# A gate projection in seven half-size products, its left operands made by quarters of x, in a hybrid decoder block on Trainium2

## The chip, the cores and the metric

The kernel runs on one core of one Trainium2 chip. The metric is the device time of one execution in microseconds. TensorE (PE in the profile; PEld is its weight load) multiplies, VectorE is DVE, ScalarE is ACT, GpSimd is POOL, SyncE is SP. Each engine works through its own queue in order. SP, ACT and POOL also issue DMA transfers.

## The reference

One decoder block over 512 positions of width 1024, in float32: a normalised input goes through one large projection, a short gated convolution and an mLSTM, whose outputs are merged. The part that the change touches is the end:

```python
merged = jax.nn.sigmoid(ga) * ya + jax.nn.sigmoid(gb) * yb
x = x + jnp.einsum('bsd,de->bse', merged, w_o[l])

gate = jax.nn.sigmoid(jnp.einsum('bsd,de->bse', rmsnorm(x, g_ple[l]), w_ple_gate[l]))
x = x + gate * jnp.einsum('bsp,pd->bsd', p[l], w_ple[l])
return rmsnorm(x, g_final)
```

So there are two 512x1024 by 1024x1024 products in a row: the output's projection (`w_o`) and the gate (`w_ple_gate`). The gate's row scale (`rsqrt` of the mean square) is applied to the product, within the sigmoid. The embedding's product `p @ w_ple` is made at the start of the kernel and kept in DRAM (`ple_d`).

## The kernel before

**Precision.** Every product is made of three passes. Each operand is cut into a high part (rounded to `float32r`, by ACT) and a low part (the rest, by DVE); `mm3` issues high x high, high x low, low x high (lines 217 to 219). So each weight block that TensorE uses costs ACT one copy and DVE one subtraction per half (`split_half`, lines 164 and 165), and each left operand the same (`cut`).

**The weights' pipeline.** A weight block is 512 rows by 512 columns, in SBUF as 128 x 4 x 512. `chunks` lists the blocks to load, `operands` the order in which TensorE uses them, with additions: `(to, c, None)` behind an operand means that, once a half of it has been cut, POOL issues a transfer that adds block `c` from DRAM into raw block `to` (line 171). Four raw buffers (`NRAW`) are filled by SP (`load_raw`, line 144); a raw buffer is free once its last cut is done. The cut halves lie in the pool `wsplit`: for each of `whi0`, `whi1`, `wlo0`, `wlo1` (high or low, first or second half) there are two buffers, taken in turn. `next_operand` hands out the next cut operand and queues the cut of the one after it (`queue_split`) as two pieces.

**The order of work.** The order on each engine is the order in which the program issues instructions. After each group of 12 matmuls (one 128x512 output tile over one block), `step(task)` calls `tick` and hands over a new task. A tick does, in this order: the first part of tasks handed over after the previous group; one weight piece; one part of every active task. A task is a generator, and each `yield` in it ends a part. So a task's first part is issued one group of matmuls later than the group that it belongs to. A temporary (`temp(tag)`) takes one of two buffers of its tag (three of tag `c`); a new one waits until all users of the old one are done, transfers too.

**Products by halves.** Most of the kernel's products use Strassen's scheme in Winograd's form (`strassen`): the left operand is cut into four quarters, the weights into four blocks, and seven products of halves, of sums and differences of these, give the result instead of eight. A product is two groups of 12 matmuls. The output's projection and the gate are not made so: each is eight products (two halves of columns by two halves of the depth, over four row tiles), 192 matmuls of 512 columns.

**The end.** During the output's projection, `add_residual` adds each result tile to x (`xr`) on DVE and squares it on ACT. As soon as half of x's columns is complete, `turn_to` transposes it on TensorE, 32 transposes of 128x128 in all (line 1135), and cuts it into `h2`, the gate's left operand. `norm_scale` makes the row scale `er`. The gate's first half of columns is handled tile by tile (`gate_embedding`: sigmoid on ACT, times embedding and plus x on DVE, square on ACT, and times `g_final` on POOL). For the second half the last row tile is split into two column halves. Each of the eight output tiles is scaled and stored from a temporary (`final`).

Of the kernel before, what the change touches and what calls it, by code (L numbers as in the profile page):

```python
# [14 lines left out]
P = 128  # L15
S = 512
# [20 lines left out]
def hybrid_block(ctx, tc, x, p, g_mix, w_in, conv_w, conv_b, w_a_out, b_gates, g_head,  # L37
# [87 lines left out]
    for view in (w_o_v, w_pg_v):  # L125
        for n in range(2):
            block(view, [(n * CW, CW)], (HC, 0) if view is w_o_v and n == 0 else (0, HC))

    last_use = {}
    for i, (r, add) in enumerate(operands):  # L130
# [23 lines left out]

    def split_tiles(i, h):

        parts = [wsplit.tile([P, HH, CW], F32R, name=f"w{u}{i}{h}", tag=f"w{u}{h}", align_bytes=256)
                 for u in ("hi", "lo")]
# [20 lines left out]

    def queue_split():  # L180
        i = state["split"]
        if i < len(operands):
            state["split"] = i + 1
            pieces.extend((i, h) for h in range(2))
# [814 lines left out]

    ya = []  # L1000
    mp_ctx, mp = open_pool("merge")
    m = mp.tile([P, NT, D], F32, name="m", tag="m")
# [117 lines left out]
    strassen(units, sink_heads, groups=2)  # L1120
    close(wb_ctx, sg_ctx)

    def turn_to(dst, src, n, scale):

        ks = range(n * HC, (n + 1) * HC)
        yield
        pts = {}
        for i in range(3):
            if i > 0:
                for k in ks[2 * i - 2:2 * i]:  # L1130
                    cut(dst[0][:, k, :], dst[1][:, k, :], pts[k], scale[:, k:k + 1])
            for k in ks[2 * i:2 * i + 2]:
                pts[k] = ps_x.tile([P, S], F32, name="ptk", tag="x")
                for t in range(NT):
                    pe.transpose(pts[k][:, t * P:(t + 1) * P], src[:, t, k * P:(k + 1) * P], ident)  # L1135
            yield


    ep_ctx, ep = open_pool("end")
    h2_ctx, h2p = open_pool("h2", side="right")  # L1140
    h2 = [h2p.tile([P, KT, S], F32R, name=f"h2_{i}", align_bytes=256) for i in range(2)]
    xr = ep.tile([P, NT, D], F32, name="xr")
    gfin = ep.tile([P, D], F32, name="gfin")
    ple = ep.tile([P, NT, D], F32, name="ple")
    ess = ep.tile([P, NT, 2], F32, name="ess")
    etot = ep.tile([P, NT], F32, name="etot")
    er = ep.tile([P, NT], F32, name="er")
    etmp = [ep.tile([P, NT], F32, name=f"etmp{i}") for i in range(3)]
    half = [slice(0, CW), slice(CW, D)]

    def load_end():
# [5 lines left out]
        for t in range(NT):  # L1157
            yield
            nc.gpsimd.dma_start(ple[:, t, :], ple_d[:, t, :])
        nc.gpsimd.dma_start(gfin, g_final.partition_broadcast(P))  # L1160
# [12 lines left out]
    ends = load_end()  # L1173
    next(ends)
    active.append(ends)
    post = add_residual(0)
    pss = [None] * NT
    w = {}
    for c, ts in ((1, (0, 1)), (0, (0, 1)), (1, (2, 3)), (0, (2, 3))):
        if c not in w:  # L1180
            w[c] = next_operand(len(w) == 0)
        for t in ts:
            if c == 1:
                pss[t] = bank(t)
            for kt in range(HC):
                mm3(pss[t], [u[:, c * HC + kt, t * P:(t + 1) * P] for u in mg], [u[kt] for u in w[c]],
                    c == 1 and kt == 0, c == 0 and kt == HC - 1)
            if (c, t) == (1, 3):
                queue_split()
            step(post(t, pss[t]) if c == 0 else None)  # L1190
    active.append(turn_to(h2, xr, 0, gp))
    block_tm([(mg, 0), (mg, HC)], add_residual(1))
    active.append(turn_to(h2, xr, 1, gp))

    def norm_scale():
        yield
        a, r, e = etmp
        dve.tensor_tensor(etot, ess[:, :, 0], ess[:, :, 1], ALU.add)
        dve.tensor_scalar(a, etot, 1.0 / D, EPS, ALU.mult, ALU.add)
        pool.tensor_tensor(r, a, mhalf, ALU.pow)  # L1200
        yield
        newton(e, a, r)
        dve.tensor_tensor(er, r, e, ALU.mult)

    active.append(norm_scale())
    fss = ep.tile([P, NT, 4], F32, name="fss")
    xg = mp.tile([P, NT, D], F32, name="xg", tag="m")[:, :, half[0]]

    def gated(ps, t, c):

        sl = xr[:, t, c]
        g = temp("e")[:, :c.stop - c.start]
        act.activation(g, ps, AF.Sigmoid, scale=er[:, t:t + 1])
        dve.tensor_tensor(g, g, ple[:, t, c], ALU.mult)
        dve.tensor_tensor(sl, sl, g, ALU.add)

    def squares(t, c, i):
        act.activation(temp("c")[:, :c.stop - c.start], xr[:, t, c], AF.Square, accum_out=fss[:, t, i:i + 1])

    def gate_embedding(t, ps):  # L1220
        gated(ps, t, half[0])
        yield
        squares(t, half[0], 0)
        pool.tensor_tensor(xg[:, t, :], xr[:, t, half[0]], gfin[:, half[0]], ALU.mult)

    block_tm([(h2, 0), (h2, HC)], gate_embedding)

    base = ep.tile([P, NT], F32, name="base")
    wl = []

    def last_part(t, cs, a, b, ps):
        for c in cs:
            if c == len(wl):
                wl.append(next_operand())
            for kt in range(HC):
                mm3(ps[:, :b - a], [u[:, c * HC + kt, t * P:(t + 1) * P] for u in h2],
                    [u[kt][:, a:b] for u in wl[c]], c == 0 and kt == 0, c == 1 and kt == HC - 1)
            tick()

    fs = ep.tile([P, NT], F32, name="fs")  # L1240

    def power(t, i):
        a, r, _ = (u[:, t:t + 1] for u in etmp)
        dve.tensor_scalar(a, fss[:, t, i:i + 1], 1.0 / D, base[:, t:t + 1], ALU.mult, ALU.add)
        pool.tensor_tensor(r, a, mhalf[:, :1], ALU.pow)

    def final_scale(t):
        a, r, e = (u[:, t:t + 1] for u in etmp)
# [3 lines left out]

    def final(t, n, on_act=False):

        y = temp("sv"[n], "y")
        f = fs[:, t:t + 1]
        if n:
            dve.scalar_tensor_tensor(y, xr[:, t, half[1]], f, gfin[:, half[1]], ALU.mult, ALU.mult)
        elif on_act:
            act.activation(y, xg[:, t, :], AF.Copy, scale=f)  # L1260
        else:
            dve.tensor_scalar(y, xg[:, t, :], f, None, ALU.mult)
        (nc.scalar if on_act else nc.sync).dma_start(out[0, t * P:(t + 1) * P, half[n]], y)

    pss = [bank(t) for t in range(NT)]
    for t in range(2):
        last_part(t, [0], 0, CW, pss[t])
    drain()
    for t in range(3):
        last_part(t, [1] if t < 2 else [0, 1], 0, CW, pss[t])  # L1270
    psl = ps_x.tile([P, S], F32, name="mml", tag="x")
    last_part(3, [0, 1], 0, CW // 2, pss[3])
    last_part(3, [0, 1], CW // 2, CW, psl)
    dve.tensor_scalar(base, fss[:, :, 0], 1.0 / D, EPS, ALU.mult, ALU.add)
    q = [slice(CW, CW + CW // 2), slice(CW + CW // 2, D)]
    gated(pss[0], 0, half[1])
    squares(0, half[1], 1)
    power(0, 1)
    gated(pss[1], 1, half[1])
    squares(1, half[1], 1)  # L1280
    power(1, 1)
    final_scale(0)
    for n in range(2):
        final(0, n)
    final_scale(1)
    for n in range(2):
        final(1, n)
    gated(pss[2], 2, half[1])
    squares(2, half[1], 1)
    power(2, 1)  # L1290
    gated(pss[3][:, :CW // 2], 3, q[0])
    squares(3, q[0], 1)
    final_scale(2)
    final(2, 1)
    gated(psl[:, :CW // 2], 3, q[1])
    final(2, 0, True)
    squares(3, q[1], 2)
    dve.tensor_scalar(base[:, 3:4], fss[:, 3, 1:2], 1.0 / D, base[:, 3:4], ALU.mult, ALU.add)
    power(3, 2)
    final_scale(3)  # L1300
    final(3, 0, True)
    final(3, 1)
    close(ep_ctx, mp_ctx, hp_ctx, tp_ctx, h2_ctx)


_INS = ["x", "p", "g_mix", "w_in", "conv_w", "conv_b", "w_a_out", "b_gates", "g_head",
# [19 lines left out]
```

## Time and profile before

| what | value |
|---|---|
| median of 3 runs | 857.89 us (857.46 to 858.75) |
| the profiled execution | 858.12 us |
| its span | 856.3 us |
| PE busy | 845.6 us (99%) |
| DVE busy | 630.3 us (74%) |
| ACT busy | 483.4 us (56%) |
| POOL busy | 218.1 us (25%) |
| granted TensorE clock, mean | 0.997 |

The span runs from the first to the last instruction of the core; the time of an execution is a little longer. A row of the order of time reads: start in us, duration in us, engine, line, operation, output <- inputs, and in brackets how long the engine was idle before it and what ended that. `x2` means that two like rows were merged, and the duration is then that of both together. In a group's row, `busy, mean ns` stand ahead of the idle time. Matmuls overlap, so their step, start to start, is shorter than their duration.

### The profile page before, as it was taken

What the parts mean: (1) busy time and instruction counts of PE and PEld (TensorE: products, weight loads), DVE (VectorE), ACT (ScalarE), POOL (GpSimd) and SP (SyncE); (2) the same over time, 40 slices, a digit from 0 to 9 for tenths busy, and PEclk for the clock granted to TensorE, in tenths of its full rate; (3) what the DMA queues carried; (4) which work ended last, traced back from release to release, by engine and by line L of the source; (5) the groups of instructions that cost most, each with busy time, mean ns of one, the idle gap of its engine ahead of it and who ended that gap; (6) DMA issues with size and microseconds to landing.
All of it is one profiled execution on the core that took longest, in us unless ns stands there. A gap on an engine that the chain in (4) does not pass through costs nothing.

```text
span 856.3 us, 12144 instructions
## 1 busy us (share of the span) xinstructions
PE 845.6 (99%) x4658; PEld 735.4 (86%) x4658; DVE 630.3 (74%) x813; ACT 483.4 (56%) x702; POOL 218.1 (25%) x221
## 2 busy tenths in 40 slices
PE   8999999999999999999999999999999999999996
PEld 6888888887889988888888999999998888888885
DVE  6786667976777676788677779897885788964465
ACT  6477665657755566665766654545543256634343
POOL 5103222203224332220223333342410222130031
PEclk9999999999999999999999999999999999999998
DMA  9749669779958998796998689999998487884002
GB/s 313 267 136 179 161 129 220 196 265 238 267 117 205 243 220 183 180 214 197 266 236 218 137 218 179 184 179 185 181 359 291 83 200 190 222 323 145 1 1 98
DMA packets 100139, 167.58 MB, mean 196 GB/s; under 512 B 5421, under 2 KB 45921, under 8 KB 98801
## 3 DMA queue, kind: packets, MB, share of 16 engines
q0 software_dynamic: 38672, 70.86, 43.0%
q1 hardware_dynamic: 58544, 90.97, 32.3%
q10 hardware_dynamic: 2864, 4.98, 1.6%
q8 instruction: 36, 0.59, 0.3%
q14 instruction: 23, 0.18, 0.1%
HBM read 150.01 MB, written 16.78 MB: 195 GB/s over the span
## 4 chain that ended last, share of the span: by engine, by line
PE 95%; DVE 2%; DMA 1%; issue 1%; ACT 1%; SPq 0%; POOL 0%; POOLq 0%; ACTq 0%
PE mm L217 29%; PE mm L218 29%; PE mm L219 29%; PE pv L217 1%; PE pv L219 1%; PE pv L218 1%; DMA xin<-in_x 1%; PE pty L799 1%; PE sc L219 1%; PE sc L218 1%; PE sc L217 1%; PE ptk L1135 0%; PE pth L1102 0%; PE pt L536 0%; DVE xin L531 0%
## 5 line engine op out<-in xcount | busy, mean ns | idle before, releaser
L165 DVE TENSOR_TENSOR wlo<-wraw,whi 128x1024 fp32r<-128x1024 f32 x238 | 298.3, 1256 | 118.6 <-ACT whi L164 117.8
L164 ACT ACTIVATE whi<-wraw 128x1024 fp32r<-128x1024 f32 x240 | 251.1, 1054 | 103.4 <-PE mm L219 44.5
L171 POOL DMA_DIRECT2D wraw<-in_w_in x112 | 136.7, 1418 | 316.9 <-DVE wlo L165 244.4
L333 ACT ACTIVATE s<-mm 128x512 f32<-128x512 f32 x84 | 50.2, 598 | 100.9 <-PE mm L219 99.6
L217 PE MATMUL mm<-whi,hs 128*128 128x512 f32 x256 | 99.9, 390 | 0.0
L218 PE MATMUL mm<-wlo,hs 128*128 128x512 f32 x256 | 99.8, 390 | 0.0
L219 PE MATMUL mm<-whi,hs 128*128 128x512 f32 x256 | 99.7, 389 | 0.0
L217 PE MATMUL mm<-hn_hi,whi 128*128 128x256 f32 (+1 forms) x304 | 93.4, 307 | 0.0
L219 PE MATMUL mm<-hn_hi,wlo 128*128 128x256 f32 (+1 forms) x304 | 93.0, 306 | 0.0
L218 PE MATMUL mm<-hn_lo,whi 128*128 128x256 f32 (+1 forms) x304 | 92.9, 306 | 0.0
L217 PE MATMUL mm<-hs,whi 128*128 128x256 f32 x320 | 90.9, 284 | 0.0
L218 PE MATMUL mm<-hs,whi 128*128 128x256 f32 x320 | 90.5, 283 | 0.0
L219 PE MATMUL mm<-hs,wlo 128*128 128x256 f32 x320 | 90.5, 283 | 0.0
L217 PE MATMUL mm<-whi,hn_hi 128*128 128x512 f32 x192 | 75.3, 392 | 0.0
L218 PE MATMUL mm<-wlo,hn_hi 128*128 128x512 f32 x192 | 75.0, 390 | 0.0
L219 PE MATMUL mm<-whi,hn_lo 128*128 128x512 f32 x192 | 74.7, 389 | 0.0
L218 PEld LDWEIGHTS mm<-hs,whi 128*128 128x128 f32 x320 | 61.4, 192 | 0.0
L217 PEld LDWEIGHTS mm<-hs,whi 128*128 128x128 f32 x320 | 61.4, 192 | 0.0
L219 PEld LDWEIGHTS mm<-hs,wlo 128*128 128x128 f32 x320 | 61.4, 192 | 0.0
L219 PEld LDWEIGHTS mm<-hn_hi,wlo 128*128 128x128 f32 x304 | 58.1, 191 | 2.8 <-POOL wlo L165 0.3
L218 PEld LDWEIGHTS mm<-hn_lo,whi 128*128 128x128 f32 x304 | 58.1, 191 | 2.4
L217 PEld LDWEIGHTS mm<-hn_hi,whi 128*128 128x128 f32 x304 | 58.1, 191 | 2.4
(306 smaller groups left out, 1673.7 us busy)
## 6 DMA issues: line engine op xcount, KB each, us to landing
wraw<-in_w_in SPq DMA_DIRECT2D x32, 1024.0 KB, 5.5
wraw<-in_w_in POOLq DMA_DIRECT2D x52, 512.0 KB, 7.7
wraw<-in_w_in SPq DMA_DIRECT2D x48, 512.0 KB, 5.4
wraw<-in_w_in POOLq DMA_DIRECT2D x60, 256.0 KB, 6.0
wraw<-in_w_b_out SPq DMA_DIRECT2D x7, 1024.0 KB, 6.4
wraw<-in_w_b_out POOLq DMA_DIRECT2D x12, 512.0 KB, 6.7
yt_d<-yc POOLq DMA_DIRECT2D x4, 1024.0 KB, 4.9
wraw<-in_w_a_out SPq DMA_DIRECT2D x4, 1024.0 KB, 5.5
```

What stands on the lines that cost most here:

```text
L164: act.activation(hi, t, AF.Copy)
L165: (e_lo or dve).tensor_tensor(lo, t, hi.bitcast(F32), ALU.subtract)
L171: nc.gpsimd.dma_start(raws[to][:, ks, cs], src[:, ks, :], accum_op=ALU.add)
L217: pe.matmul(ps, lhsT=a[0], rhs=b[0], start=first, stop=False, **kw)
L218: pe.matmul(ps, lhsT=a[0], rhs=b[1], start=False, stop=False, **kw)
L219: pe.matmul(ps, lhsT=a[1], rhs=b[0], start=False, stop=last, **kw)
L333: act.activation(to[i], src, AF.Copy, scale=scale)
L799: pe.transpose(pts[v][:, t * P:(t + 1) * P], y[:, t, v * P:(v + 1) * P], ident)
```

## The change

The gate's weights become four blocks with additions: seven operands with four additions, in the manner of `strassen` (`g11`, `g21`, `g22`, `g12`; row half, column half). The first operand (`early`) is cut during the output's projection into a buffer of its own, in the merged values' place, and `queue_split` steps over it.

The output's projection now finishes row tiles 0 and 1 before 2 and 3 for both column halves. After each pair of tiles, `lefts(h, n)` transposes a quarter of x (row half h, column half n) on TensorE, copies it to SBUF with the scale `g_ple` on ACT (`quarter`), and makes sums, differences and cuts: `g_a11`, `g_s3` (after the second quarter), `g_a22`, `g_s1`, `g_s2` (third), `g_a12`, `g_s4` (fourth).

The gate is then a loop over six products of two groups (products 0 to 5 in the text, with operands 0 to 5), and a last product (with operand 6) in four groups of 256 columns, with the gates' reads between them. `keep_acc` and `g2` copy an accumulator to a temporary (ACT); `g1`, `g3`, `g5` add a temporary and a bank (DVE), take the sigmoid (ACT), and multiply by the embedding (DVE). For row tiles 2 and 3 (`g1`, `g3`) a transfer issued by POOL adds the product to `xr` (`by_dma`); two groups later ACT squares the sum. For tiles 0 and 1 DVE adds. The embedding is loaded after product 0, into the place of operand 0's cut. The order of the last outputs is new: tiles 2, 3, 0, 1, with `xg` (times `g_final`, on POOL) for two of them.

The diff, cut to its core:

```diff
+    early = len(operands)
+    g11, g21, g22, g12 = (chunk(w_pg_v, k, [(n * CW, CW)]) for k, n in ((0, 0), (HC, 0), (HC, 1), (0, 1)))
+    operands.extend([(g11, [(g11, g12, None)]), (g11, [(g11, g22, None)]), (g21, [(g12, g22, None)]),
+                     (g11, [(g11, g21, None)]), (g22, []), (g12, []), (g11, [])])
+    own = {}
...
     def queue_split():
         i = state["split"]
+        if i in own:
+            i += 1
...
+    def cut_early():
+        for _ in range(5):
+            yield
+        own[early] = mp.tile([P, 2, HC, CW], F32R, name="wearly", tag="m", align_bytes=128)
+        pieces.extend((early, h) for h in range(2))
...
+    def quarter(h, n, to):
+        pts = [ps_x.tile([P, S], F32, name="ptk", tag="x") for _ in range(2)]
+        at = [pts[i // 2][:, i % 2 * H2:(i % 2 + 1) * H2] for i in range(HC)]
+        for i in range(HC):
+            for t in range(2):
+                k = n * HC + i
+                pe.transpose(at[i][:, t * P:(t + 1) * P], xr[:, 2 * h + t, k * P:(k + 1) * P], ident)
+        yield
+        for i in range(HC):
+            k = n * HC + i
+            act.activation(to[i // 2][:, i % 2, :], at[i], AF.Copy, scale=gp[:, k:k + 1])
...
+    def lefts(h, n):
...
+        else:
+            u = hp.tile([P, 2, 2, HC, H2], F32R, name="glb", tag="qk", align_bytes=256)
+            for i, to in enumerate((g_a12, g_s4)):
+                to.extend(u[:, i, v] for v in range(2))
+            yield from quarter(h, n, v1)
+            cut(*g_a12, b1)
+            yield
+            dve.tensor_tensor(b1, b2, b1, ALU.subtract)
+            cut(*g_s4, b1)
...
+    for n, cs in ((0, (1, 0)), (1, (0, 1))):
...
+                    if c == cs[0] and t == 3:
+                        queue_split()
+                    step(post(t, pss[t]) if c == cs[1] else None)
...
+    def embed(c, t, cols, by_dma=False):
+        sl = xr[:, t, cols]
+        dve.tensor_tensor(c, c, ple[t][:, cols], ALU.mult)
+        if by_dma:
+            nc.gpsimd.dma_start(sl, c, accum_op=ALU.add)
+        else:
+            dve.tensor_tensor(sl, sl, c, ALU.add)
...
+    def snap(to, i, tag, src):
+        to[i] = temp(tag)
+        act.activation(to[i], src, AF.Copy)
+        yield
+    def from_two(c, ps):
+        dve.tensor_tensor(c, c, ps, ALU.add)
+        return c
+    def keep_acc(i):
+        yield from snap(sn, i, "s", acc[i])
+    def g1(i):
+        t = 2 + i
+        c = from_two(sn[i], bb[i])
+        act.activation(c, c, AF.Sigmoid, scale=er[:, t:t + 1])
+        yield
+        embed(c, t, half[0], True)
+        yield
+        yield
+        squares(t, half[0], 0)
+        add_base(t, 0)
+    def g2(i):
+        yield from snap(sv, i, "v", cc[i])
...
+    def g5(i):
+        t = i
+        c = from_two(sv[i], acc[i])
+        act.activation(c, c, AF.Sigmoid, scale=ner[:, t:t + 1])
+        yield
+        embed(c, t, half[1])
+        squares(t, half[1], 0)
+        pool.tensor_tensor(xg[t], xr[:, t, half[1]], gfin[:, half[1]], ALU.mult)
+        add_base(t, 0)
+
+    for left, banks, tag, post in ((g_a11, acc, order[0], keep_acc), (g_s1, cc, order[1], g2), (g_a12, bb, "x", g1),
+                                   (g_s2, acc, None, keep_acc), (g_s4, cc, None, g3), (g_s3, acc, None, g5)):
+        w = next_operand()
+        for i in range(2):
+            if tag:
+                banks[i] = ps_x.tile([P, S], F32, name="mmb", tag="x") if tag == "x" else bank(i, tag)
+            for kt in range(HC):
+                mm3(banks[i], [u[:, kt, i * P:(i + 1) * P] for u in left], [u[kt] for u in w],
+                    bool(tag) and kt == 0, kt == HC - 1, skip_group_check=not tag)
+            step(post(i))
+        if banks is acc and tag:
+            load_ple()
...
+    last_part(0, 0)
+    tick()
+    last_part(1, 0)
+    tick()
+    drain()
+    gated(0, 0)
+    last_part(0, 1)
+    gated(1, 0)
+    squares(0, q[0], 1)
+    add_base(0, 1)
+    last_part(1, 1)
+    gated(0, 1)
+    squares(1, q[0], 1)
+    add_base(1, 1)
+    gated(1, 1)
+    squares(0, q[1], 2)
+    final_scale(2)
+    final(2, 0)
+    power(0, 2)
+    squares(1, q[1], 2)
+    final(2, 1)
+    power(1, 2)
+    final_scale(3)
+    final(3, 0)
+    final_scale(0)
+    final(0, 1, True)
+    final(0, 0)
+    final_scale(1)
+    final(1, 1, True)
+    final(1, 0)
+    final(3, 1)
```

`g3` is like `g1` with `cc[i]`, the negative scale `ner`, the second half of columns, and `power(t, 1)` in place of `add_base`.

More of the change, by code (lines that the diff above doesn't have):

```diff
@@ L155, in split_tiles @@
     def split_tiles(i, h):
-        parts = [wsplit.tile([P, HH, CW], F32R, name=f"w{u}{i}{h}", tag=f"w{u}{h}", align_bytes=256)
-                 for u in ("hi", "lo")]
+        if i in own:
+            parts = [own[i][:, v, HH * h:HH * h + HH, :] for v in range(2)]
+        else:
+            parts = [wsplit.tile([P, HH, CW], F32R, name=f"w{u}{i}{h}", tag=f"w{u}{h}", align_bytes=256)
+                     for u in ("hi", "lo")]
         splits.setdefault(i, []).append(parts)
@@ L1121, in hybrid_block @@
     close(wb_ctx, sg_ctx)
[L1123 to L1136, printed above, removed]
     ep_ctx, ep = open_pool("end")
-    h2_ctx, h2p = open_pool("h2", side="right")
-    h2 = [h2p.tile([P, KT, S], F32R, name=f"h2_{i}", align_bytes=256) for i in range(2)]
+    gl_ctx, glp = open_pool("gate_lhs", side="right")
     xr = ep.tile([P, NT, D], F32, name="xr")
     gfin = ep.tile([P, D], F32, name="gfin")
-    ple = ep.tile([P, NT, D], F32, name="ple")
     ess = ep.tile([P, NT, 2], F32, name="ess")
@@ new lines, in left_pair, with by_two, two_temps @@
+    def left_pair(pool_, tag=None):
+        u = pool_.tile([P, 2, HC, H2], F32R, name="gl", tag=tag, align_bytes=256)
+        return [u[:, v] for v in range(2)]
+    g_a11, g_s3, g_s1, g_a22, g_s2 = (left_pair(glp, f"gl{i}") for i in range(5))
+    g_a12, g_s4 = [], []
+    fx = ep.tile([P, 2, HC, H2], F32, name="fx", tag="fx", align_bytes=256)
+    b1, b2 = (fx[:, v] for v in range(2))
+    def by_two(u):
+        return [u[:, 2 * i:2 * i + 2, :] for i in range(2)]
+    def two_temps(name):
+        return [temp("e", name).rearrange("p (f s) -> p f s", f=2) for _ in range(2)]
@@ L1168, in post @@
             yield
-        return post
[L1173 to L1193, printed above, removed]
+            if t % 2:
+                yield from lefts(t // 2, n)
+        return post
     def norm_scale():
+        yield
         yield
@@ L1205, in hybrid_block @@
     active.append(norm_scale())
     fss = ep.tile([P, NT, 4], F32, name="fss")
[L1207 to L1218, printed above, removed]
@@ L1245, in power, with add_base @@
         pool.tensor_tensor(r, a, mhalf[:, :1], ALU.pow)
+    def add_base(t, i):
+        to = base[:, t:t + 1]
+        dve.tensor_scalar(to, fss[:, t, i:i + 1], 1.0 / D, to if i else EPS, ALU.mult, ALU.add)
     def final_scale(t):
@@ L1275, in hybrid_block @@
[L1275 to L1281, printed above, removed]
+    acc, bb, cc, sn, sv = ([None, None] for _ in range(5))
+    def snap(to, i, tag, src):
+        to[i] = temp(tag)
+        act.activation(to[i], src, AF.Copy)
+        yield
+    def from_two(c, ps):
[3 more added lines that the diff above has]
+        yield from snap(sn, i, "s", acc[i])
@@ new lines, in g5 @@
+    def g5(i):
+        t = i
+        c = from_two(sv[i], acc[i])
+        act.activation(c, c, AF.Sigmoid, scale=ner[:, t:t + 1])
+        yield
+        embed(c, t, half[1])
[5 more added lines that the diff above has]
+        w = next_operand()
+        for i in range(2):
+            if tag:
+                banks[i] = ps_x.tile([P, S], F32, name="mmb", tag="x") if tag == "x" else bank(i, tag)
+            for kt in range(HC):
+                mm3(banks[i], [u[:, kt, i * P:(i + 1) * P] for u in left], [u[kt] for u in w],
[3 more added lines that the diff above has]
+            load_ple()
+        if left is g_s4:
+            u = ep.tile([P, 2, CW], F32, name="xg", tag="fx", align_bytes=256)
+            xg.extend(u[:, t, :] for t in range(2))
@@ L1285, in hybrid_block @@
+    final(0, 0)
     final_scale(1)
[L1286 to L1301, printed above, removed]
+    final(1, 1, True)
```

124 lines of the change are left out of this document (83 added, 41 removed).

## The prediction

> **What bounds the kernel now.** I read the page's head, then busy time by stretches of time, then the instructions of the gate stage in order of time.
>
> ```profile
> span 856.3 us, 12144 instructions
> PE 845.6 (99%) x4658; PEld 735.4 (86%) x4658; DVE 630.3 (74%) x813; ACT 483.4 (56%) x702; POOL 218.1 (25%) x221
> ...
> PE 95%; DVE 2%; DMA 1%; issue 1%; ACT 1%; SPq 0%; POOL 0%; POOLq 0%; ACTq 0%
> ```
>
> ```profile
> 800.00:820.00 20.00, 20.00 (x98) 16.74 (x97) 9.70 (x17) 8.59 (x13) 1.03 (x1) 1.00 0.00 0
> 820.00:840.00 20.00, 20.00 (x90) 16.53 (x90) 14.14 (x16) 9.02 (x19) 7.39 (x5) 1.00 0.00 1
> 850.00:857.00 7.00, 0.00 (x0) 0.00 (x0) 1.50 (x5) 0.94 (x3) 0.54 (x1) 0.57 0.30 114
> ```
>
> From the chain that ended last, a group of transposes; from the order of time, TensorE's gate matmuls (start, duration):
>
> ```profile
> 784.41 0.87 PE ptk L1135 x8
> ```
>
> ```profile
> 802.37 0.39 PE L217 MATMUL mm<-whi,h 128*128 128x512 f32 x1
> ...
> 842.03 0.39 PE L219 MATMUL mm<-whi,h 128*128 128x512 f32 x1
> 842.26 0.28 PE L217 MATMUL mm<-whi,h 128*128 128x256 f32 x1
> ...
> 847.89 0.28 PE L219 MATMUL mml<-whi,h 128*128 128x256 f32 x1
> ```
>
> TensorE never waits in the gate (columns of a stretch: length, then PE, PEld, DVE, ACT, POOL busy, clock, DMA share, GB/s). 168 matmuls of 512 columns start between 802.37 and 842.03; less two groups of eight transposes at 0.87 us that is 37.92 us in 167 steps, 0.227 us each. The last 48, of 256 columns, step by 5.63/47 = 0.12 us. DVE is busy for 23.8 of the 40 us and ACT for 17.6, so both have time to spare, and DMA none to do. The tail, from 848.0 to 856.3, is 8.3 us without matmuls.
>
> **The change: the gain.** Seven products of 24 matmuls take the place of eight: 24 x 0.227 = 5.4 us less on TensorE. Transposes stay at 32; three groups instead of two lie ahead of the gate, so product 0 starts at 802.37 + 0.87 = 803.3, and with the fourth group behind it product 1 starts at 809.6. Unhindered, product 2 follows at 815.0 and the last matmul ends at 842.6.
>
> **Parts that I cost at nothing.** The four gate loads stay. Eight accumulating loads of 512 KB are new, on an idle DMA and POOL; each is issued at least five groups of twelve matmuls (13.6 us) before the piece that reads it, and landing takes 7.7 (row below). The embedding's loads move behind product 0 on POOL's queue (809) and are due at 833. Operand 0 is cut early, into the merge buffer, and the first left operands under the output projection, where ACT and DVE idle. If that cover were gone, each piece would cost ACT 1.05 and DVE 1.22 us (rows below).
>
> **The costs are waits in ACT's and DVE's queues,** which run in program order. Durations:
>
> ```profile
> 773.62 1.06 ACT L164 ACTIVATE whi<-wraw 128x1024 fp32r<-128x1024 f32 x1 [0.31 <-PE mm L219]
> 780.42 1.99 ACT L164 ACTIVATE whi<-wraw 128x1024 fp32r<-128x1024 f32 x2
> 781.49 2.36 DVE L165 TENSOR_TENSOR wlo<-wraw,whi 128x1024 fp32r<-128x1024 f32 x2 [1.80 <-ACT whi L164]
> 740.85 0.60 ACT L333 ACTIVATE s<-mm 128x512 f32<-128x512 f32 x1 [3.02 <-PE mm L219]
> 834.30 0.69 ACT L1213 ACTIVATE e<-mm,er 128x512 f32<-128x512 f32 x1 [4.35 <-PE mm L219]
> 835.02 0.69 DVE L1214 TENSOR_TENSOR e<-e,ple 128x512 f32<-128x512 f32 x1 [2.60 <-ACT e L1213]
> 836.54 0.63 ACT L1218 ACTIVATE c<-xr 128x512 f32<-128x512 f32 x1 [1.54 <-DVE xr L1215]
> 837.07 0.19 ACT L1218 ACTIVATION_READ_ACCUMULATOR c<-xr 128x1 f32 x1
> 845.79 0.46 ACT L1213 ACTIVATE e<-mm,er 128x256 f32<-128x256 f32 x1
> 846.28 0.42 DVE L1214 TENSOR_TENSOR e<-e,ple 128x256 f32<-128x256 f32 x1
> 810.88 0.17 DVE L234 TENSOR_SCALAR etmp<-etmp 128x4 f32<-128x4 f32 x1
> 811.08 0.16 DVE L1203 TENSOR_TENSOR er<-etmp,etmp 128x4 f32<-128x4 f32 x1
> ...
> 851.75 0.75 DVE L1258 SCALAR_TENSOR_TENSOR y<-xr,fs,gfin 128x512 f32<-128x512 f32 x1
> ```
>
> A weight piece is 1.05 us on ACT (0.94 to the next in a row) and 1.22 on DVE; a snapshot 0.60; a sigmoid 0.69; a 512-wide DVE operation 0.69; a square 0.82 with its read; a small one 0.2; a hand-over (834.30 + 0.69 to 835.02) 0.03. For the quarter copies, 256 wide, I take a 0.37 us step, an estimate from the 0.46 row (bounds 0.3 and 0.46).
>
> *First wait: product 2.* Because operand 0 has a buffer of its own, the queue of pieces runs one operand further ahead: during product 1 operand 3 is cut, whose buffer operand 1 still holds. Its first piece is in ACT's queue ahead of the last quarter's copies. As at 773.62, it waits for the matmul that frees the half: the 18th of product 1, 809.6 + 4.1 + 0.14 = 813.8. Then ACT has four copies to 816.4 and the high part of `g_a12` to 817.4, DVE the low part to 818.7. Product 2's third matmul needs that: product 2 starts at 818.3 instead of 815.0, **+3.3**.
>
> *Then a chain.* ACT: snapshot, operand 3's second piece to 818.9; DVE to 820.1, five small ones to 821.0, `b2 - b1` to 822.3; ACT `g_s4` to 823.4, DVE to 824.6; ACT operand 4 to 824.8, DVE to 826.1. Then DVE's sum for the first result, ACT's sigmoid, ACT's piece and DVE's piece follow one another (0.69 + 0.69 + 1.05 + 1.22, 3.5 with overlaps, in a group of 2.7), twice: 829.6, 833.1. DVE multiplies by the embedding to 833.7 and POOL issues an accumulating transfer from that temporary into `xr`.
>
> *Second wait: the snapshot.* The temporary is one of only two with tag `s`. ACT's next snapshot, one group later, takes the same buffer; so ACT waits until the transfer has landed; operands 5 and 6 are behind it in ACT's queue, and product 5 overwrites the accumulator that it reads. Nothing like it is in the trace of before; nearest rows (one line's accumulating transfers of 256 KB from 560 to 640 us; POOL's plain stores of 256 KB; the page's DMA issues):
>
> ```profile
> L171 POOL DMA_DIRECT2D wraw<-in_w_in x20: 1203/1421/1749, 562.1 to 617.7; - x20
> ...
> DMA to landing us min/median/max: 4.4/5.8/6.7
> ```
>
> ```profile
> L683 POOL DMA_DIRECT2D qk_d<-qk_s x4: 539/544/625, 40.9 to 49.0; - x4
> ...
> DMA to landing us min/median/max: 2.7/3.8/5.5
> ```
>
> ```profile
> wraw<-in_w_in POOLq DMA_DIRECT2D x52, 512.0 KB, 7.7
> ...
> wraw<-in_w_in POOLq DMA_DIRECT2D x60, 256.0 KB, 6.0
> ...
> out<-y ACTq DMA_DIRECT2D x2, 256.0 KB, 2.4
> ```
>
> Ends: 2.7 and 6.0. I take 4.4, the quickest accumulating one of this size, as DMA is idle here. So: landing 833.7 + 4.4 = 838.1, snapshot 838.7, product 5 starts at 838.8 instead of 834.6, **+4.2**. Operand 5's second piece: ACT 839.7, DVE 840.9, second multiply 841.5, landing 846.0, second snapshot 846.6, which product 5's second half waits for: **+5.1**. ACT operand 6 to 847.5, a square to 848.3, DVE's base 848.9, sum 849.6, sigmoid 850.3, piece 851.3 and 852.5, base and sum 853.3, multiply 853.9 (third transfer), sum 854.5. The last product overwrites what this sum read: it starts at 854.6 instead of 849.4, **+5.2**.
>
> *Third wait.* The third transfer lands at 858.4; behind it in the queues: square 859.2, power, multiply and add for row tile 0 to 860.8, square 861.7, base and power 862.5, multiply and add for tile 1 to 863.95, square 864.8. Only then come the last gates. The last product's second half stands behind the first of their reads, at 865.1 instead of 857.5: **+7.7**; it could start earlier and the end would be the same, since the queues set it. Matmuls end at 868.0.
>
> *Tail.* Sigmoid 868.7, multiply and add to 869.6, then on DVE alone fourteen small operations and six final products (0.75, of which 0.1 overlaps) for tiles 2, 3, 0, 1. The last two use buffers of earlier outputs and wait for their stores (2.4): 877.8, against 852.5 now (851.75 + 0.75); add the same 3.8 to the end. Tail 13.6 instead of 8.3: **+5.3**.
>
> Sum: -5.4 + 3.3 + 4.2 + 5.1 + 5.2 + 7.7 + 5.3 = +25.4, a span of 881.7. The profiled execution took 858.12 us, 1.8 beyond its span, and the median of the runs is 857.89, 0.2 less: **883 us**.
>
> [...]
>
> **Rivals.**
> *A smaller slip.* The transfers land in 2.7: three times 1.7 less, 878. Or ACT starts without the first lag: operand 5's first piece is freed at 820.5 + 4.2 = 824.7, so the multiply ends at 827.7 instead of 833.7, six less: 877. Both: 872. For it: the 2.4 and 2.7 rows. Against: they write without reading, and the first lag follows from queue order.
> *Everything hidden (not slower).* Product 5 starts unhindered at 831.4 if its snapshot starts by 830.8: with the multiply at 827.7 the transfer must land within 3.1 us, which decides it. Then matmuls end at 842.6, the tail is 13.6, and the span 856.2: 858 us, no change; without the waits for output buffers (1.6) 856.4. For it: DVE and ACT have 16 and 22 us idle in 40. Against: the idle time is not where the chain is, and 4.4 is over 3.1.
> *A slower clock.* The stretch from 850 on has a granted clock of 0.57 where TensorE idles. If its pauses of 4 to 8 us bring that, the last two groups take 1.4 us longer each: +2.9, 886; with 6.0 us landings (+4.8) 891. Against: no pause between matmuls in the trace shows it. [...]
>
> **How the numbers follow.** Forecast (878 to 891, slower clock included at 0.15): 0.63; smaller slip 0.22; hidden 0.13, of which half below 0.2%, which is about what a measurement of this kernel can tell from no change; 0.02 beyond. The range leaves out the hidden case and the 0.02: 868 to 891. Faster 0.07, same 0.07, slower 0.86.
>
> **What would show it.** Right: DVE's product with the embedding followed by ACT idle until a transfer into `xr` lands; TensorE idle ahead of `g_a12` (about 3 us) and before product 5 and 6; POOL's transfers landing in 4 to 5 us; two output products waiting on stores. Wrong: TensorE at 20.0 of 20 us until 842, or ACT's snapshots running on time.

## The result and the profile after

| kernel | median, us | range, us | profiled span, us |
|---|---|---|---|
| before | 857.86 | 857.46 to 858.75 | 856.3 |
| changed | 882.78 | 882.73 to 882.93 | 881.1 |

The changed kernel takes 1.0289 times as long (95% interval 1.0271 to 1.0307), 24.9 us more; 883 was forecast. The page's head and the shares of the chain that ended last (here it could be followed back over the last 40 us alone, to a transfer into `xr`, so its shares are small):

```profile
span 881.1 us, 12187 instructions
...
PE 851.4 (97%) x4634; PEld 738.7 (84%) x4634; DVE 642.9 (73%) x835; ACT 500.8 (57%) x734; POOL 229.2 (26%) x231
...
DVE 1%; DMA 1%; ACT 1%; PE 1%; issue 0%; ACTq 0%; DVEq 0%
```

TensorE has 24 matmuls fewer, as forecast, and its busy time is nevertheless 5.8 us longer. The same stretches as before the change, with one more for the end:

```profile
800.00:820.00 20.00, 17.63 (x76) 13.68 (x75) 13.37 (x16) 12.37 (x20) 8.92 (x9) 0.94 0.96 219
820.00:840.00 20.00, 17.78 (x73) 14.34 (x72) 9.61 (x15) 7.50 (x9) 2.14 (x2) 0.93 0.34 57
840.00:860.00 20.00, 12.69 (x45) 10.33 (x44) 8.92 (x17) 8.66 (x17) 4.70 (x5) 0.70 0.23 39
860.00:870.00 10.00, 5.49 (x24) 5.20 (x24) 5.48 (x16) 4.00 (x13) 2.20 (x2) 0.66 0.00 0
```

In the gate, where TensorE was busy for 20.0 of 20 us, it now stands still for 2 to 7 us in each stretch, DVE does more than before from 800 to 820 (13.4 instead of 9.7 us) and less from 820 to 840 (9.6 instead of 14.1), and the granted clock falls to 0.7. No engine is full; the order of the queues holds them up, as the experiments below show. The pauses, one row each (the bracket says how long the engine was idle ahead of the row, and what ended it), from the order of time of the weight loads, of ACT and of DVE:

```profile
817.65 0.29 PEld L227 LDWEIGHTS mmb<-whi,glb 128*128 128x128 f32 x1 [2.75 <-ACT glb L234]
838.32 0.29 PEld L227 LDWEIGHTS mm<-whi,gl 128*128 128x128 f32 x1 [2.65 <-ACT s L1330]
845.39 0.29 PEld L227 LDWEIGHTS mm<-whi,gl 128*128 128x128 f32 x1 [2.99 <-ACT s L1330]
853.14 0.29 PEld L227 LDWEIGHTS mm<-whi,gl 128*128 128x128 f32 x1 [3.77 <-ACT s L1357]
862.74 0.29 PEld L227 LDWEIGHTS mm<-whi,gl 128*128 128x128 f32 x1 [4.41 <-ACT eq L1401]
```

```profile
814.00 1.06 ACT L172 ACTIVATE whi<-wraw 128x1024 fp32r<-128x1024 f32 x1 [1.37 <-PE mm L229]
814.96 1.55 ACT L1194 ACTIVATE fx<-ptk,prm 128x256 f32<-128x256 f32 x4
...
837.67 0.60 ACT L1330 ACTIVATE s<-mm 128x512 f32<-128x512 f32 x1 [5.58 <-DMA xr<-s]
...
844.74 0.60 ACT L1330 ACTIVATE s<-mm 128x512 f32<-128x512 f32 x1 [5.53 <-DMA xr<-s]
...
865.71 0.47 ACT L1401 ACTIVATE eq<-mm,er 128x256 f32<-128x256 f32 x1 [1.50 <-PE mm L229]
...
868.27 0.47 ACT L1401 ACTIVATE eq<-mm,er 128x256 f32<-128x256 f32 x1 [1.69 <-PE mm L229]
```

```profile
833.27 0.69 DVE L1291 TENSOR_TENSOR s<-s,ple 128x512 f32<-128x512 f32 x1
...
877.33 0.75 DVE L1322 SCALAR_TENSOR_TENSOR y<-xr,fs,gfin 128x512 f32<-128x512 f32 x1 [1.28 <-DMA out<-y]
```

ACT's piece of operand 3 does wait for TensorE at 814.0 with the quarter copies behind it. DVE's product with the embedding ends at 833.96; ACT sits idle for 5.6 us ahead of its snapshot (the copy of an accumulator), until the transfer made from that product has landed, 3.7 us after the product's end; product 5 starts behind the snapshot. The last two rows of ACT show what the sum didn't have: ACT waits for the last product's matmuls. They step by 0.21 us, where the kernel before had 0.12. The granted clock (third number from the end) in four stretches, each beginning with the first matmul behind a pause:

```profile
817.60:821.00 3.40, 3.31 (x7) 2.21 (x8) 3.03 (x7) 1.43 (x2) 2.54 (x3) 0.51 0.73 119
838.30:841.50 3.20, 3.18 (x8) 2.53 (x9) 1.83 (x2) 0.91 (x1) 0.13 (x1) 0.50 0.00 0
845.30:848.50 3.20, 3.11 (x8) 2.50 (x9) 1.89 (x3) 1.86 (x5) 0.00 (x0) 0.52 0.00 0
862.70:868.20 5.50, 5.46 (x24) 5.20 (x24) 2.71 (x8) 1.73 (x6) 0.16 (x1) 0.50 0.00 0
```

### The profile page after: what moved, and what is told of

It is laid out like the page before. It is cut to its first block, busy times and chain, and to the rows that moved or that the text cites. A ratio compares the mean times of both kernels' runs of the same rounds, so it can differ in the third digit from the quotient of the medians.

```text
span 881.1 us, 12187 instructions
## 1 busy us (share of the span) xinstructions
PE 851.4 (97%) x4634; PEld 738.7 (84%) x4634; DVE 642.9 (73%) x835; ACT 500.8 (57%) x734; POOL 229.2 (26%) x231
## 5 line engine op out<-in xcount | busy, mean ns | idle before, releaser
L173 DVE TENSOR_TENSOR wlo<-wraw,whi 128x1024 fp32r<-128x1024 f32 x242 | 302.4, 1251 | 134.3 <-ACT whi L172 133.8
L172 ACT ACTIVATE whi<-wraw 128x1024 fp32r<-128x1024 f32 x244 | 255.3, 1054 | 106.4 <-PE mm L229 53.1
```

The source lines that it names most:

```text
L172: act.activation(hi, t, AF.Copy)
L173: (e_lo or dve).tensor_tensor(lo, t, hi.bitcast(F32), ALU.subtract)
```

## The experiments

Theory: two buffer waits and a queue order make TensorE pause, and the second halves of the last product reach the end because they run at half the clock (0.50 from 862.70 to 868.20) behind a pause. Rivals: DVE and ACT are full whatever the order; the landings alone; the time lost is made good anyway. The runs of the kernel before beside these had medians of 858.06 and 858.11 us.

### One part at a time, from the changed kernel

**e1: other buffers for the second snapshots.** Tag `e` has two buffers that nothing uses at that time.

```diff
-        yield from snap(sn, i, "s", acc[i])
+        yield from snap(sn, i, "s" if sn[i] is None else "e", acc[i])
```

> The second pair of snapshots of the accumulator takes buffers with tag e, which nothing uses at that time, in place of the two with tag s, from which POOL's accumulating transfers still read. Nothing else changes. Theory (the second wait is the buffer): ACT no longer waits for a landing (11.1 us in two waits in the changed kernel), the second snapshots start within 1 us of the end of product 3's halves, product 5 starts 3 to 4 us sooner, and the span falls by about 9 us: 874 us, between 870 and 877. Rival (ACT and DVE are simply full with their hand-overs, and the wait only fills time that they would lose anyway): less than 2 us fall, 881 or more. Rival (half-clock matmuls at the end are part of the loss and come from the pauses): with shorter pauses the last 48 matmuls also get quicker, 1 to 3 us beyond the 9.

Measured: 874.01 us, 1.0186 of before (1.0169 to 1.0203), 8.8 less than the changed kernel. Pauses are left at three places: product 2, and the two halves of the last product. ACT's snapshots, and the weight loads behind a pause:

```profile
831.84 0.58 ACT L1330 ACTIVATE e<-mm 128x512 f32<-128x512 f32 x1
...
833.27 0.58 ACT L1330 ACTIVATE e<-mm 128x512 f32<-128x512 f32 x1
```

```profile
817.65 0.19 PEld L227 LDWEIGHTS mmb<-whi,glb 128*128 128x128 f32 x1 [2.76 <-ACT glb L234]
818.91 0.19 PEld L229 LDWEIGHTS mmb<-whi,glb 128*128 128x128 f32 x1 [0.96 <-DVE glb L235]
843.92 0.25 PEld L227 LDWEIGHTS mm<-whi,gl 128*128 128x128 f32 x1 [3.82 <-ACT e L1357]
853.52 0.29 PEld L227 LDWEIGHTS mm<-whi,gl 128*128 128x128 f32 x1 [5.18 <-ACT eq L1401]
```

The snapshots come 5.8 and 11.5 us sooner and product 5 has no pause left. The second wait is the buffer, and of the edits that were tried one at a time this one gives the most. Some half a us of the 8.8 is the clock's: the last product's second half takes 5.0 us instead of 5.5, and ACT's last two gates, each waiting for matmuls, start 2.01 us apart (856.49, 858.50) instead of 2.56. That the clock is back at full ahead of the end is an estimate from these times.

**e2: no transfer, DVE adds.** The buffers stay two.

```diff
-        embed(c, t, half[0], True)
+        embed(c, t, half[0])
...
-        embed(c, t, half[1], True)
+        embed(c, t, half[1])
```

> The four additions of the gated embedding into xr are made by DVE right behind the product instead of by POOL's accumulating transfers. The snapshots keep their two buffers. Theory (what costs is the landing of 3.3 us plus POOL's issue, since the buffer is held so long): a buffer is free 0.7 us after the product instead of 3.7, which takes about 3 us from each of the three landings on the path and gives 0.7 back for each of four additions on DVE: about 6 us less, 877 us, between 873 and 880. Rival (DVE is the bound in this stretch, so 2.8 us more of work on it cancels the gain): 881 to 885.

Measured: 877.55 us, 1.0227 (1.0212 to 1.0242), 5.2 less. From the waits (us in total, times, longest):

```profile
ACT s L1330 <- DVE xr L1295: 5.2, 2, 2.6
```

ACT's waits at the snapshot are 2.6 us each, now for DVE's addition into `xr`, instead of 5.6. So the price of the transfer is its landing, seen through the buffer; 2.8 us more work on DVE costs less than that.

**e3 and e4: the cuts without their lead**, from the changed kernel and from e1. The lead is that the queue of weight pieces runs one operand further ahead.

```diff
-                    if c == cs[0] and t == 3:
+                    if c == cs[0] and t == 3 and n == 0:
```

> The extra call that queues the next operand's pieces is left out in the second half of the output projection, so that in the gate the operands are cut one product later than in the changed kernel, into a buffer that is already free. Theory (the first wait comes from operand 3's piece standing ahead of the last quarter's copies): ACT no longer waits for TensorE at 814, product 2 starts at about 815 instead of 818; but the landings still hold the snapshots, and the pieces behind them are now needed sooner, so product 5 starts at the same time as before, within 1 us; the last product, whose operand stands behind fewer waits, comes up to 3 us earlier. In all 878 to 883. Rival (the first lag carries through the whole chain): 3.3 us or more are gained and kept, 876 to 879 and product 5 at 835 or earlier. Rival (the lead is needed to cover the cuts): slower, 884 or more.

> Both edits: the second snapshots in buffers with tag e, and no extra lead of the cuts. Theory (the two waits together are what delays products 2 to 5): TensorE runs nearly without a stop to the end of product 5 at about 837, the rest is the queue of gates and final products behind it: 864 to 867 us, still slower than the kernel before, because the end after the matmuls is longer. If everything is hidden, 858. Rival (a third cause, the ping-pong between DVE and ACT, carries on without the waits): 870 or more.

Measured: 886.15 us (1.0327, 1.0312 to 1.0342), 3.4 more than the changed kernel, and 877.36 (1.0228, 1.0212 to 1.0243), 3.4 more than e1. My theory missed both; the rival of e3 that the lead is needed holds, and e4 lies in the range of its own rival (870 or more). Product 2 does start sooner, by 1.3 us, not 3, but the pieces come late elsewhere. From the order of time of e3, weight loads and ACT:

```profile
823.54 0.19 PEld L227 LDWEIGHTS mm<-whi,gl 128*128 128x128 f32 x1 [0.76 <-ACT whi L172]
...
827.10 0.19 PEld L227 LDWEIGHTS mm<-whi,gl 128*128 128x128 f32 x1 [1.30 <-ACT whi L172]
```

```profile
854.55 0.72 ACT L1368 ACTIVATE v<-v,ner 128x512 f32<-128x512 f32 x1 [2.49 <-DVE v L1334]
855.18 1.04 ACT L172 ACTIVATE whi<-wraw 128x1024 fp32r<-128x1024 f32 x1
858.72 0.72 ACT L1368 ACTIVATE v<-v,ner 128x512 f32<-128x512 f32 x1 [2.49 <-DVE v L1334]
```

Product 3's matmuls now wait for each cut, and operand 6's cuts stand between the last sigmoids, which ACT begins 4.5 us later (858.72, against 854.26 in the changed kernel). Taking the lead away removes the cause of the first wait and a cover together; e7 takes the cause alone.

**e5: the four parts of the last product in a row.**

```diff
     last_part(1, 0)
     tick()
+    last_part(0, 1)
+    last_part(1, 1)
     drain()
     gated(0, 0)
-    last_part(0, 1)
     gated(1, 0)
     squares(0, q[0], 1)
     add_base(0, 1)
-    last_part(1, 1)
     gated(0, 1)
```

> The changed kernel with the four parts of the last product issued one behind the other, ahead of the gates that read them, so that TensorE waits for no gate there. The rest, and the order of every other engine's work, stays. Theory (the last product's second halves run at half the clock behind a pause, and their slowness reaches the end): ACT's idle time of 1.5 and 1.7 us ahead of the last two gates goes, and the span falls by 2.6 to 3.2: 880 us, between 878.5 and 881.5. Rival (as the prediction put it: the second half could start earlier and the end would be the same, since the queues set it): 882 to 883.5.

Measured: 879.86 us, 1.0254 (1.024 to 1.0268), 2.9 less than the changed kernel. ACT's last two gates have no idle time ahead of them:

```profile
864.06 0.46 ACT L1401 ACTIVATE eq<-mm,er 128x256 f32<-128x256 f32 x1
...
864.85 0.46 ACT L1401 ACTIVATE eq<-mm,er 128x256 f32<-128x256 f32 x1
```

The matmuls still begin at half the clock (0.50 from 853 to 858), only nobody waits for them. So the prediction's words "it could start earlier and the end would be the same" are wrong for the kernel as it ran: 2.9 us of the end hung on these matmuls. The edit takes away their late start and their slowness together. That the slowness is what reached the end is worked out, not tried by itself: at 0.12 us a step the 24 matmuls would have ended at about 865.8 (862.74 + 23 x 0.12 + 0.28) instead of 868.2, an estimate of 2.4 of the 2.9 us.

### From e1, what is left

**e6: the sum one step ahead of its sigmoid** (in `g1` and `g3`), and the squares of these rows later.

```diff
         c = from_two(sn[i], bb[i])
+        yield
         act.activation(c, c, AF.Sigmoid, scale=er[:, t:t + 1])
...
         embed(c, t, half[0], True)
-        yield
-        yield
+        for _ in range(5):
+            yield
         squares(t, half[0], 0)
+        yield
         add_base(t, 0)
```

> Made from the kernel of 874.0 us (second snapshots in buffers with tag e). For the first two pairs of results the gate's sigmoid is issued one step behind DVE's sum, so that ACT cuts a piece between them and neither engine waits for the other; the first squares of these rows are issued later, behind the sigmoids, so that ACT doesn't wait for a landing. Theory (a ping-pong of DVE's sum, ACT's sigmoid, ACT's piece and DVE's piece, 3.6 us in a step of 2.7, makes operand 6 and the sums late): the last product starts 2 to 4 us earlier than 843.9, and the end moves with it: 871 us, between 870 and 872.5. Rival (the chain is set by the landings and the drain behind them, so an earlier sum changes nothing, and embeddings that come one step later cost): 873 to 876.

Measured: 869.03 us, 1.013 (1.0116 to 1.0143), 5.0 less than e1. First e1's ping-pong, DVE and ACT in turn, each waiting for the other's last instruction:

```profile
825.99 0.68 DVE L1334 TENSOR_TENSOR s<-s,mmb 128x512 f32<-128x512 f32 x1
...
826.70 0.72 ACT L1343 ACTIVATE s<-s,er 128x512 f32<-128x512 f32 x1 [1.89 <-DVE s L1334]
827.33 1.04 ACT L172 ACTIVATE whi<-wraw 128x1024 fp32r<-128x1024 f32 x1
...
828.41 1.23 DVE L173 TENSOR_TENSOR wlo<-wraw,whi 128x1024 fp32r<-128x1024 f32 x1 [1.74 <-ACT whi L172]
829.55 0.68 DVE L1334 TENSOR_TENSOR s<-s,mmb 128x512 f32<-128x512 f32 x1
```

Sum to sum takes 3.56 us (825.99 to 829.55), where the prediction had 3.5, in a group of 2.7. In e6 the pause of 3.82 us ahead of the last product is gone: it starts at 840.27, and its first 24 matmuls keep the full clock (256 columns, 0.12 us a step); the second 24 still start behind a pause, of 5.2 us, at half the clock (0.21 us a step). The gain is a little over the expected range. The edit also moves the squares, one of which made ACT wait 2.6 us for a landing in e1; how much of the 5.0 us is theirs was not tried.

**e7: the last quarter's copies ahead of the piece.** For the one step behind product 1's first half, `tick` cuts its piece last.

```diff
-        if pieces:
+        late = state.pop("late", False)
+        if pieces and not late:
             split_half(*pieces.popleft())
         active[:] = [g for g in active if not next(g, True)] + new
+        if pieces and late:
+            split_half(*pieces.popleft())
...
+            state["late"] = left is g_s1 and i == 0
             step(post(i))
```

> Made from the kernel of 874.0 us. In the one step of product 1 where the last quarter is copied, the operand's piece is issued behind the copies and the high part of g_a12 instead of ahead of them. The lead of the cuts is kept. Theory (the piece that waits for TensorE's last read at 813.8 is what delays the copies): product 2's first weights load at about 816 instead of 817.7, and 1.5 us less to the end: 872.5, between 871.5 and 873.2. Rival (the lost time at product 2 is made good later, in idle time of DVE and ACT): 873.3 to 874.5.

Measured: 871.87 us, 1.0158 (1.0142 to 1.0173), 2.1 less than e1. Product 2's first weights load at 815.96, as expected, and the pause ahead of them is 0.34 us; for the low part of `g_a12` there are 0.96 us more:

```profile
815.96 0.19 PEld L230 LDWEIGHTS mmb<-whi,glb 128*128 128x128 f32 x1 [0.34 <-ACT glb L237]
817.22 0.19 PEld L232 LDWEIGHTS mmb<-whi,glb 128*128 128x128 f32 x1 [0.96 <-DVE glb L238]
```

The first wait is what the prediction said it was, and it isn't made good later.

### All together

**e8** has e1, e6 and e7, and another end: half of row tile 0, the whole of row tile 1, the other half of row tile 0; output products of rows 2 and 3 placed earlier in the order, half of them by ACT from POOL's `xr * gfin`; buffers of their own for the outputs.

```diff
     last_part(0, 0)
     tick()
-    last_part(1, 0)
-    tick()
-    drain()
-    gated(0, 0)
-    last_part(0, 1)
...
+    for kt in range(HC):
+        mm3(acc[1], [u[:, kt, P:2 * P] for u in g_a22], [u[kt] for u in w], False, kt == HC - 1,
+            skip_group_check=True)
+    tick()
+    gated(0, q[0])
+    last_part(0, 1)
+    drain()
...
```

> All of these together: second snapshots in buffers with tag e, sigmoids one step behind the sums, copies ahead of the piece, and a new order of the end: the last product as a half of row tile 0, the whole of row tile 1 and the other half of row tile 0, the rows' squares behind their gates, the output products of rows 2 and 3 made while the last product runs, half of them by ACT, and buffers of their own for the outputs. Theory (matmuls can end at about 843 when no wait is left, and an end of 11 to 13 us is DVE's own work): 856 to 860, no change against the kernel before or a little less. If the matmuls run without a stop and the end is as short as before, 853. Rival (ACT and DVE together are the bound from product 2 on, whatever the order): 862 or more.

Measured: 862.08 us, 1.0046 (1.0033 to 1.0059). TensorE is busy for 20.00 of the 20 us from 820 to 840 at a granted clock of 1.00, and its last matmul starts at 843.04, as the theory has it. But the time is over the theory's 860 and in the rival's range (862 or more). The rival's reason, that ACT and DVE bound TensorE from product 2 on, is not what the trace shows; what is too long is the end behind the matmuls, 16.5 us (843.04 + 0.28 to 859.8) and not 11 to 13. The output products of rows 2 and 3, expected while the last product runs, begin at 849.17. DVE and POOL in order of time:

```profile
839.67 0.69 DVE L1298 TENSOR_TENSOR xr<-xr,v 128x512 f32<-128x512 f32 x1
...
841.06 3.30 DVE L1298 TENSOR_TENSOR xr<-xr,v 128x512 f32<-128x512 f32 x1
...
844.73 1.37 DVE L1298 TENSOR_TENSOR xr<-xr,eq 128x256 f32<-128x256 f32 x1
```

```profile
840.96 1.60 POOL L1374 TENSOR_TENSOR xg<-xr,gfin 128x512 f32<-128x512 f32 x1
842.22 1.57 POOL L1354 TENSOR_TENSOR xg<-xr,gfin 128x512 f32<-128x512 f32 x1
844.43 1.38 POOL L1374 TENSOR_TENSOR xg<-xr,gfin 128x512 f32<-128x512 f32 x1 [0.64 <-DVE xr L1298]
```

The same addition for another row tile takes 0.69 us, and 3.30 when two of POOL's products run: it ends 0.57 behind the second of them (842.22 + 1.57).

**e9: without POOL's four products**; DVE makes all outputs.

```diff
-        pool.tensor_tensor(xg[t], xr[:, t, half[0]], gfin[:, half[0]], ALU.mult)
...
-        pool.tensor_tensor(xg[t], xr[:, t, half[1]], gfin[:, half[1]], ALU.mult)
...
-    final(2, 0, True)
+    final(2, 0)
...
```

> Made from the kernel of 862.1 us with everything together. POOL's four products of xr with gfin are left out; DVE makes all eight output products itself (0.75 us each, in place of four on ACT). In the kernel of 862.1, DVE's addition of 128x512 took 3.30 us instead of 0.69, another of 128x256 1.37 instead of 0.42 and a product 1.56 instead of 0.69, each while POOL multiplied. Theory (POOL's product holds DVE up while both run): these three go back to 0.69, 0.42 and 0.69, 4.4 us in all, of which four more products on DVE take 2.7 back: 860.4 us, between 859 and 861.5. Rival (the three were long because they waited for something else, a transfer into xr or a buffer): they stay long, and the products come on top: 863 or more.

Measured: 860.52 us, 1.0025 (1.0015 to 1.0035). The additions are short again:

```profile
841.51 0.69 DVE L1298 TENSOR_TENSOR xr<-xr,v 128x512 f32<-128x512 f32 x1
...
842.57 0.42 DVE L1298 TENSOR_TENSOR xr<-xr,eq 128x256 f32<-128x256 f32 x1
```

So POOL's products are what made the addition take 3.30 us instead of 0.69; by what means was not shown.

**e10: an end in pairs.** The last norm's small operations for two row tiles at once; the second column half of row tiles 2 and 3 added by DVE, that of 0 and 1 by transfer; squares placed where ACT is idle.

```diff
-        embed(c, t, half[1], True)
+        embed(c, t, half[1])
...
-        embed(c, t, half[1])
+        embed(c, t, half[1], True)
...
+    dve.tensor_tensor(base[:, r23], fss[:, r23, 0], fss[:, r23, 1], ALU.add)
+    power_pair(r23)
...
+    scale_pair(r23)
...
```

> Made from the previous one, with a shorter end: the small operations of the last norm for two row tiles at once, rows 2 and 3 added by DVE (ready sooner) and the second column half of rows 0 and 1 by transfer, squares placed where ACT is idle. Matmuls end at 843 as before. Theory (DVE's own work behind 839 is the bound: 12 us, and 3 for the last store): a span of 854 to 855.5, 856 to 857.5 us, a little less than the kernel before. Rival (waits in the new order eat the gain, or the landings of the last two transfers are late): 858 to 861.

Measured: 858.13 us, 0.9998 (0.9989 to 1.0007): no difference from the kernel before, at the lower edge of the rival's range. Its span is 856.5 us. The stretch from 840 to 850, last matmul and last outputs:

```profile
840.00:850.00 10.00, 3.90 (x23) 3.26 (x21) 8.73 (x23) 5.73 (x18) 3.96 (x5) 0.81 0.52 131
```

```profile
843.62 0.28 PE L232 MATMUL mm<-whi,gl 128*128 128x256 f32 x1
```

```profile
850.59 2.74 DVE L1326 SCALAR_TENSOR_TENSOR y<-xr,fs,gfin 128x512 f32<-128x512 f32 x4
```

The gain of seven products is there: matmuls end at 843.9, 4.3 us before those of the kernel before (847.89 + 0.28). It is given back behind them: 12.6 us from the last matmul to the end of the span, instead of 8.1. DVE is busy for 8.7 of the 10 us from 840 to 850 and then makes the last four outputs in a row; ACT and TensorE are done. None of the ten kernels beats the one before.

## Why the prediction was right

The mechanism came out, and so did the time, 882.8 for 883. That the number is so close is luck: errors of 2.4, 2.6 and 0.8 us nearly cancelled. Its steps beside the trace:

| step | forecast | measured |
|---|---|---|
| operand 3's piece free at | 813.8 | 814.0 |
| product 2 starts | 818.3 | 817.65, its third matmul at 818.91 |
| product 5 starts | 838.8 | 838.32 |
| its second half | 846.6 | 845.39 |
| last product starts | 854.6 | 853.14 |
| its second half | 865.1 | 862.74 |
| matmuls end | 868.0 | 868.23 |
| last output product ends | 877.8 | 878.08 |
| span | 881.7 | 881.1 |

- *The gain of 5.4 us* was right in number of matmuls (4658 to 4634). In e10, where TensorE pauses only at product 2, matmuls end 4.3 us sooner than in the kernel before.
- *First wait*: right in cause, and in size up to product 2's third matmul. What it left out is the half clock (0.51) behind the pause: product 3 starts at 824.83, 1.1 us later than 818.3 + 24 x 0.227. It cost next to nothing, since ACT and DVE were the slower chain there: in e1, with the clock at 1.00, the first sum starts at 825.99 instead of 826.13. e7 removes the queue order and gets 2.1 us back at the end. e3 shows that the lead that causes it also covers the cuts.
- *Second wait*: right in cause (e1: 8.8 us; e2: 5.2). Its size was the term that was mis-sized: from the end of DVE's product to the snapshot I took 4.4 us, and it was 3.7. The transfers from issue to landing (median):

```profile
xr<-s POOLq DMA_DIRECT2D x4, 256.0 KB, 3.3
```

The row I took, 4.4 to 6.7, was for transfers that fetch from HBM while others run (DMA share 0.95 from 560 to 640 us). The accumulating transfers from SBUF to SBUF here landed in 3.3 (3.2 to 3.3; DMA share 0.34 from 820 to 840, 0.23 from 840 to 860), within my bounds of 2.7 and 6.0. Three landings, 0.7 to 0.8 less each, make 2.2 of the 2.4 us by which the last product's second half came sooner.
- *Third wait*: the place was right, the words "the queues set it" were not. The second half took 5.5 us instead of 2.9, and e5 shows that 2.9 of the end hung on when it ended. That is the rival of the slower clock, priced at +2.9 (24 steps of 0.12 us twice as long; the trace of before has a clock of 0.50 from 851 to its end, with TensorE idle) and given 0.15: it happened together with the forecast, and was left out of the sum. My argument against it, that no pause between matmuls in the trace of before shows such a thing, was none: that trace has no pause there.
- *Tail*: 9.8 us from the last matmul to the last output product was forecast, 9.85 measured, with both outputs waiting for stores as said; behind it came 3.0 us, not 3.8.
- *What cancelled*: landings -2.4, clock +2.6, the last store -0.8.
- *Everything hidden*: the rival gave 858 where no wait is left. With the waits taken away one by one the time is 858.1 (e10), although the landing (3.3) is over the 3.1 from which I let that case begin: it took other buffers and another order, which the change doesn't have. So the equal number is a coincidence and no test of that rival: it had matmuls end at 842.6 and 13.6 us behind them, e10 has 843.9 and 12.6.
- *A smaller slip* didn't come about: the first product with the embedding ended at 833.96, forecast 833.7, and the landing was between that rival's 2.7 and my 4.4.

## What to carry to other kernels

When a tuned kernel saves matmuls, look at what the other engines do in the shorter time: here every added wait was one engine's queue holding work for another behind an instruction that waited for a buffer, a transfer or its partner. A temporary that is the source of a transfer is in use until the transfer lands (ACT waited 5.6 us for one here); give the next user another buffer before anything else (8.8 us for another tag). And a tail counts as much as the matmuls ahead of it: saved time at TensorE is worth nothing if the engine that finishes has that much more left to do (e10: 4.3 us sooner, 12.6 us behind the matmuls instead of 8.1).

## What was not expected of the hardware

- The same pause was followed by half the clock in one kernel and by the full clock in another. Product 2's first matmul, and the stretch behind it, in the changed kernel (the stretch is the first of the four above) and in e1:

```profile
817.65 0.80 PE L227 MATMUL mmb<-whi,glb 128*128 128x512 f32 x1 [2.33 <-ACT glb L234]
```

```profile
817.65 0.50 PE L227 MATMUL mmb<-whi,glb 128*128 128x512 f32 x1 [2.33 <-ACT glb L234]
817.60:821.00 3.40, 2.82 (x11) 2.04 (x12) 3.02 (x7) 1.43 (x3) 2.54 (x3) 1.00 0.79 125
```

Behind the same 2.33 us at the same place the clock was 0.51 in one and 1.00 in the other (in e6 too the weights behind this pause load in 0.19 us each, as in e1, where the changed kernel takes 0.29 to 0.34). Read in steps of 0.1 us, the changed kernel's clock falls at 817.67, 838.15, 844.98, 851.80 and 862.04 and is back 3.41, 3.41, 3.41, 6.83 and 6.83 us later; 20.48, 6.83, 6.82 and 10.24 us lie between the falls. Why the same pause did it in one kernel and not in the other was not shown.
- A slow stretch in the changed kernel's gate took 3.41 or 6.83 us: the last product's second 24 matmuls ran at 0.50 for all of their 5.5 us, and its first 24 for all of their 5.45 (853.17 to 858.62).
- DVE's addition of two tensors in SBUF was held up while POOL multiplied: 3.30 us for 0.69 (e8), and 0.69 again without POOL's work (e9).
